# Sum of reciprocals: 127 rows a partition, and the last 128 rows loaded early onto chosen partitions

## The chip, the core and the metric

The kernel runs on one core of a Trainium2 chip. The metric is the device time of one execution in microseconds (us): the median of several runs. Lower is better.

## The reference

```python
batch, seq, dim = 32, 512, 1024
x = np.abs(np.random.randn(batch, seq, dim)).astype(np.float32) + 1e-6

def reference(x):
    return np.sum(1.0 / x, axis=-1).astype(np.float32)
```

There are 32 x 512 = 16,384 rows of 1,024 numbers (4,096 bytes a row, 67.1 MB in all). Each row gives one sum of reciprocals.

## The kernel before

**Layout.** 128 partitions hold 128 rows each: partition p has rows 128 p to 128 p + 127 of x. "Row r" below is the r-th row of all partitions at once, a 128 x 1,024 tile of 512 KB. A load (line 187, issued by SyncE, SP) brings one or several rows into `ring`, which has space for R = 40 rows; row r sits in place r % 40. The last two rows are loaded as halves (256 KB each), numbered 126 to 129. The ring is all the buffering there is: a load into a place waits until the row there before has been used up.

**Arithmetic.** A row is cut into halves a and b of 512 columns. Since 1/a + 1/b = (a + b) / (a b), one reciprocal serves two numbers. The reciprocal is made on ScalarE as exp(-ln(S a b)) with S = 2^17, and the factor S is put back in the last step. For every row there are these steps, each a letter in the plan:

- P (line 199): the product a b on GpSimd (POOL), mostly of two rows in one instruction, into a slot of `prod`. Some rows have it on VectorE (DVE, line 220) instead: W reads both halves from the ring, V reads b from PSUM, where a TensorE matmul with the identity (C, line 209) has copied it.
- L (line 242): Ln on ScalarE (ACT), in place in `prod`.
- E (line 251): Exp on ScalarE, in place, or into a bank of PSUM.
- S (line 232): for a part of the rows, two matmuls with the identity add a + b in a PSUM bank.
- R (line 267): one DVE instruction multiplies and sums. With S it takes (a + b) from PSUM and the reciprocal from `prod` (512 columns); without S it takes a and b from the ring and the reciprocal from PSUM (1,024 columns). It writes the row's sum into a column of `sums`, and frees the ring.

**Order.** `PLAN` is a list of some 500 such steps, written out by hand or by a planner; D is a load of so many rows. Every engine does its own steps in the order of the list. Loads are large at first (2, 10, 14, 14, 11, 9 rows) and small at the end (single rows, then halves), so that compute, which begins late, can catch up. The helper `note` keeps the waits between engines few. SP's loads use eight semaphores in turn, so a load also waits for the landing of the load eight places before it.

**Output.** When the sums of the first DONE = 114 columns are there, six stores of 19 columns go out (line 289), and a last one of 14 columns at the end (line 291).

Of the kernel before, what the change touches and what calls it, by code (L numbers as in the profile page):

```python
# [11 lines left out]
def kernel(  # L12
# [7 lines left out]
    P = 128  # L20
    D = 1024
    H = D // 2
    F = 128
    R = 40
    NP = 22
    LAST = F - 2
    DONE = 114
    S = float(2**17)

    PLAN = """
        D2 D10 D14 D14 P0+2 C3@3 S2@0 V3 P2 L0+2@0 C11@3 S3@1 E0+2@6 P4+2 V11 L2+2@2 R0 S6@2
        E2+2 R1 P6+2 L4+2@4 R2 R3 E4+2@6 S7@0 P8+2 L6+2@8 R4 S10@1 E6+2 R5 P10 L8+2@10 R6 R7  # L40
        S11@2 E8+2@6 L10+2@6 R8 E10+2 R9 D11 R10 R11 P12+2 C19@3 S14@0 V19 P14+2 L12+2@12
        S15@1 E12+2@6 S18@2 R12 P16+2 L14+2@16 R13 E14+2 R14 P18 L16+2@18 R15 S19@0 E16+2@6
        P20+2 L18+2@14 R16 S22@1 E18+2 R17 D9 P22+2 L20+2@20 R18 R19 E20+2@6 S23@2 P24+2
        L22+2@0 R20 E22+2 R21 L24+2@2 R22 R23 E24+2@6 P26 C27@3 R24 S26@0 P28+2 V27 R25 D7
        L26+2@4 C35@3 E26+2 S27@1 P30+2 V35 L28+2@8 R26 S30@2 R27 E28+2@6 P32+2 L30+2@10 R28
        S31@0 E30+2 R29 P34 L32+2@12 S34@1 R30 R31 E32+2@6 P36+2 S35@0 L34+2@6 R32 E34+2 R33
        D7 P38+2 S38@2 L36+2@16 R34 R35 E36+2@6 S39@1 P40+2 L38+2@18 R36 C43@3 E38+2 R37 D6
        S42@0 P42 L40+2@14 V43 R38 E40+2@6 P44+2 R39 S43@2 L42+2@20 R40 E42+2 S46@1 R41 D3
        P46+2 L44+2@0 R42 R43 E44+2@6 S47@0 P48+2 L46+2@2 R44 S50@2 E46+2 R45 P50 L48+2@4
        R46 C51@3 R47 E48+2@6 S51@1 P52+2 V51 R48 D6 L50+2@8 C59@3 E50+2 R49 P54+2 S54@0  # L50
        L52+2@10 V59 R50 E52+2@6 R51 S55@2 P56+2 L54+2@12 R52 E54+2 S58@1 R53 D5 P58
        L56+2@16 R54 R55 E56+2@6 S59@0 P60+2 L58+2@6 R56 S62@2 E58+2 R57 D4 P62+2 L60+2@14
        R58 R59 E60+2@6 S63@1 P64+2 L62+2@18 R60 S66@0 E62+2 R61 D4 P66 L64+2@20 R62 C67@3
        R63 E64+2@6 P68+2 S67@2 V67 R64 L66+2@0 S70@1 R65 D4 E66+2 P70+2 L68+2@2 R66 R67
        S71@0 E68+2@6 P72+2 L70+2@4 R68 D3 E70+2 R69 D2 C75@3 P74 L72+2@10 S74@2 R70 V75
        P76+2 E72+2@6 R71 S75@1 L74+2@8 R72 D2 E74+2 R73 D2 P80 S78@0 L76+2@12 R74 P81
        L80@16 R75 S79@2 E76+2@6 P78+2 L81@17 R76 D2 S81@1 E80@5 E81 R80 L78+2@6 W82 E78+2
        R81 R77 D1 D1 D1 D1 D1 P88 C85@6 S85@1 R78 P83 L88@18 V85 E88@7 R79 P84 S84@0
        L82+2@14 R88 E82+2@5 P86+2 L84+2@19 R82 D1 E84+2 R83 D1 D1 D1 C90@7 P91 L86+2@0
        S91@2 R85 P93 V90 E86+2@5 R84 P92 S90@1 L90+2@2 R87 L93@21 W89 L92@10 R86 D1 D1 D1  # L60
        D1 E93@7 P94 S97@0 E92@6 R93 E90+2 P97 S94@3 L89@11 R92 E89@7 P95 L97@8 R91 S95@4
        E97 R90 L94+2@4 W96 R97 P101 C99@6 L96@9 R89 E94+2 S100@0 P98 V99 E96@5 L101@12 R95
        P100 S99@1 L98@13 R96 E101@7 L99+2@16 R101 E98@6 P104 C103@5 R94 E99+2 S105@2 R98
        P102 L104@18 V103 E104@7 W105 L102+2@6 R100 P107+2 C106@6 L105@14 R104 E102+2@4
        S108@0 V106 E105 R102 L106+3@19 P109 S107@3 R103 P110 E106+3 R105 S106@4 R99 P111+2
        L109+2@0 R107 S112@1 R108 E109+2@6 R106 L111+2@10 P114 R109 S111@0 E111+2 R110 P113
        L114@15 R111 C115@7 P116 L113@2 R112 E114@6 V115 E113@5 S117@0 P117 R114 L116@3
        L115@8 P118 E116@7 R113 S118@1 E115@6 P119 L117+2@12 R116 E117+2 R115 P120 S120@2
        L119@9 R117 P121 L120@4 S121@3 R118 E119@7 E120 R119 P122 L121@5 S122@0 E121 R120
        P123 L122@18 R121 E122 W124 L123@6 R122 L124@7 W125 S125@1 E123@7 E124@6 R123 P126  # L70
        L125@14 P127 L126@16 S127@0 R124 E125 P128 L127@17 S128@2 E126@7 P129 R125 E127
        S129@3 L128@19 R126 L129@20 E128 R127 E129 R128 R129
    """.split()

    Ln = mybir.ActivationFunctionType.Ln
    Exp = mybir.ActivationFunctionType.Exp
    mult = mybir.AluOpType.mult
    add = mybir.AluOpType.add

    x_v = x.flatten_outer_dims().rearrange("(p f) d -> p f d", p=P)  # L80
    out_v = out.flatten().rearrange("(p f) -> p f", p=P)

    act_sets = list(get_activation_tables(nc.m.arch).keys())
    nc.scalar.add_instruction(  # L84
# [13 lines left out]
    prod = pool.tile([P, NP, H], f32)  # L98
    sums = pool.tile([P, F], f32)
    ident = pool.tile([P, P], f32)  # L100
    ps = pspool.tile([P, 8, H], f32)
    make_identity(nc, ident)

# [28 lines left out]
    begun = {}  # L132
    count = {}

    def note(engine, inst, reads=(), writes=()):
        inst = inst.ins
        known = dict(begun.get(engine, {}))
        before = {}
        for spaces, writing in ((reads, False), (writes, True)):
            for space in spaces:  # L140
                for other in history.get(space, ()):
                    if writing or other[3]:
                        before[other[0].name] = other
        needed = sorted(before.values(), key=lambda o: -o[4])
        for other in needed:
            o_inst, o_engine, o_tick, _, _, o_known = other
            if o_engine == engine:
                continue
            if o_tick <= known.get(o_engine, 0):
                tc.declare_no_dep(inst, o_inst, reason="implied by other waits")  # L150
                continue
            for e, t in o_known.items():
                known[e] = max(known.get(e, 0), t)
            known[o_engine] = max(known.get(o_engine, 0), o_tick)
        count[engine] = count.get(engine, 0) + 1
        begun[engine] = known
        entry = (engine, count[engine])
        if engine == "SP":
            entry = (f"load {count[engine]}", 1)
        for spaces, writing in ((reads, False), (writes, True)):  # L160
            for space in spaces:
                history.setdefault(space, []).append(
                    (inst, *entry, writing, sum(count.values()), known)
                )
# [10 lines left out]
    def slots(r, n):  # L175
        return [("slot", pslot[q]) for q in range(r, r + n)]

    with tc.manual_schedule():
        for op, r, n, b in ops:
            p = pslot.get(r)  # L180
            if op == "D":
                n, r = r, loaded
                while n:
                    q, at, w = place(r)
# [59 lines left out]
            elif op == "E":  # L244
                pg = prod[:, p : p + n, : place(r)[2]]
                rc = pg
                if b is not None:
                    rc = ps[:, b : b + n, : place(r)[2]]
                    for j in range(n):
                        bank[r + j] = b + j  # L250
                inst = nc.scalar.activation(out=rc, in_=pg, func=Exp, scale=-1.0)  # L251
                if b is None:
                    note("ACT", inst, writes=slots(r, n))
                else:
                    banks = [("bank", b + j) for j in range(n)]
                    note("ACT", inst, slots(r, n), banks)
            elif op == "R":
                q, at, w = place(r)
                other = ps[:, bank[r], :w]
                if r in halves:  # L260
                    row = prod[:, p, :w]
                else:
                    row = ring[:, q % R, at : at + 2 * w]
                    row = row.rearrange("p (h e) -> p h e", h=2)
                    other = other.unsqueeze(1).to_broadcast([P, 2, w])
                total = sums[:, q : q + 1]
                inst = nc.vector.tensor_tensor_reduce(  # L267
                    out=row,
                    in0=row,
                    in1=other,  # L270
                    scale=S,
                    scalar=total if q in summed else 0.0,
                    op0=mult,
                    op1=add,
                    accum_out=total,
                )
                summed.add(q)
                note(
                    "DVE",
                    inst,  # L280
                    [("bank", bank[r])],
                    slots(r, 1) if r in halves else rows(r, 1),
                )

                left.discard(r)
                if not left:
                    for c in range(0, DONE, DONE // 6):
                        part = slice(c, min(c + DONE // 6, DONE))
                        nc.sync.dma_start(out=out_v[:, part], in_=sums[:, part])
                    left.add(-1)  # L290
        nc.sync.dma_start(out=out_v[:, DONE:], in_=sums[:, DONE:])
# [30 lines left out]
```

## Time and profile before

| | us |
|---|---|
| median of 3 runs | 168.01 (167.95 to 168.02) |
| span of the profiled execution, first to last instruction | 166.3 |
| busy time, PE / DVE / ACT / POOL | 132.5 / 128.3 / 132.3 / 128.2 |
| DMA packets, per DMA engine | 95.6% of the span |
| POOL product, two rows (2 x 512 columns) | 2.34 |
| DVE product, 512 columns | 0.69 |
| DVE R, 512 / 1,024 columns | 0.68 / 1.21 |
| ACT pass, 512 / 1,024 columns | 0.61 / 1.06 |
| PE matmul 128 x 512 at full clock | 0.43 |

The profiled execution has no time of its own beside its span; the median of the runs is 1.7 us above the span, which is what lies around the first and the last instruction. The profile's rows name an engine, a line and the tiles (out<-in); "idle before" is an engine's idle time ahead of an instruction with what ended it. A DMA's issue is on SP, its data move on 16 DMA engines, and a load has landed when all sixteen have reported.

### The profile page before, as it was taken

To read this page: it belongs to the slowest core of one execution; us is meant where nothing else is said; L and a number is where in the kernel's file an instruction comes from. 1 tells how busy PE (TensorE), PEld (TensorE's weight loads), DVE (VectorE), ACT (ScalarE), POOL (GpSimd) and SP (SyncE) were. 2 spreads that over 40 slices of the span, in tenths; PEclk is the share of its full clock that TensorE was granted. 3 is DMA by queue.
4 is the path that set the end of the run, shared out by engine and by line. 5 is a ranking of instruction groups with operands and counts; after the bars stand their busy time and mean duration, and the time that the engine had idled before them with its cause. 6 is when DMAs were issued, how large, how long until landed. Compare 5 with 4: busy or idle time off the path is not lost.

```text
span 166.3 us, 1348 instructions
## 1 busy us (share of the span) xinstructions
PE 132.5 (80%) x292; PEld 55.2 (33%) x292; DVE 128.3 (77%) x282; ACT 132.3 (80%) x157; POOL 128.2 (77%) x81
## 2 busy tenths in 40 slices
PE   0000799978855999999999999988699979989982
PEld 0000333333312444444343433324234424433351
DVE  0000119885787699898998898989899999999994
ACT  3040073949995899999799999996999999999992
POOL 1500795069995999999999999948977869999860
PEclk9999999999996999999999999999999999999999
DMA  5999999999998989999999999999999999999940
GB/s 189 536 394 394 441 441 441 441 441 441 441 441 349 509 368 446 430 417 438 441 434 434 406 426 446 429 424 424 414 437 437 414 410 428 410 409 410 400 139 4
DMA packets 5768, 67.26 MB, mean 404 GB/s; under 512 B 1536, under 2 KB 1536, under 8 KB 3200
## 3 DMA queue, kind: packets, MB, share of 16 engines
q1 hardware_dynamic: 5760, 67.18, 95.6%
q8 instruction: 2, 0.03, 0.1%
q14 instruction: 6, 0.05, 0.1%
HBM read 67.11 MB, written 0.07 MB: 404 GB/s over the span
## 4 chain that ended last, share of the span: by engine, by line
DMA 57%; PE 18%; ACT 8%; DVE 6%; POOL 6%; issue 3%; SPq 1%; ACTq 0%; POOLq 0%; DVEq 0%
DMA ring<-in_x_dram 57%; PE ps L232 15%; POOL prod L199 6%; ACT prod L242 4%; PE ps L209 3%; ACT ps L251 2%; DVE ring L267 2%; DVE prod L267 2%; ACT prod L251 2%; DVE prod L220 1%; SPq L187 1%; DVE sums L267 0%; ACTq L242 0%; POOLq L199 0%; DVEq L317 0%
## 5 line engine op out<-in xcount | busy, mean ns | idle before, releaser
L199 POOL TENSOR_TENSOR prod<-ring 128x1024 f32<-128x1024 f32 (+2 forms) x75 | 127.5, 1727 | 33.5 <-DMA ring<-in_x_dram 27.1
L232 PE MATMUL ps<-ring,ident 128*128 128x512 f32 (+1 forms) x260 | 116.9, 596 | 5.2 <-DVE sums L267 4.5
L242 ACT ACTIVATE prod<-prod 128x1024 f32<-128x1024 f32 (+2 forms) x78 | 68.5, 892 | 24.9 <-DVE prod L220 14.3
L267 DVE CUSTOM_DVE_ANT_1 ring<-ring,ps 128x1024 f32<-128x1024 f32 (+1 forms) x65 | 76.4, 1208 | 8.9 <-ACT ps L251 8.7
L232 PEld LDWEIGHTS ps<-ring,ident 128*128 128x128 f32 x260 | 49.2, 193 | 71.7 <-issue 51.6
L267 DVE CUSTOM_DVE_ANT_0 prod<-prod,ps 128x512 f32<-128x512 f32 (+1 forms) x63 | 40.9, 677 | 0.4 <-PE ps L232 0.4
L209 PE MATMUL ps<-ring,ident 128*128 128x512 f32 x32 | 19.3, 689 | 25.7 <-DMA ring<-in_x_dram 24.0
L251 ACT ACTIVATE ps<-prod 128x1024 f32<-128x1024 f32 (+2 forms) x41 | 34.1, 838 | 4.5 <-DVE sums L267 3.7
L251 ACT ACTIVATE prod<-prod 128x1024 f32<-128x1024 f32 (+3 forms) x37 | 34.4, 931 | 0.9
L220 DVE TENSOR_TENSOR prod<-ring,ps 128x512 f32<-128x512 f32 x16 | 10.9, 684 | 26.3 <-PE ps L209 26.3
L209 PEld LDWEIGHTS ps<-ring,ident 128*128 128x128 f32 x32 | 6.0, 213 | 36.0 <-issue 21.4
L267 DVE DVE_READ_ACCUMULATOR2_ANT sums<- 128x1 f32 x130 | 10.7, 82 | 0.0
L220 DVE TENSOR_TENSOR prod<-ring 128x512 f32<-128x512 f32 x6 | 4.1, 688 | 0.1
L84 ACT ACT_TABLE_LOAD x1 | 1.3, 1283 | 0.7 <-PEq L306 0.7
L267 DVE CUSTOM_DVE_ANT_0 prod<-prod,ps,sums 128x256 f32<-128x256 f32 x2 | 0.9, 475 | 0.0
masks.py:197 POOL MEMSET ident<- 128x128 f32 x1 | 0.2, 204 | 0.3 <-POOLq L306 0.3
masks.py:199 POOL TENSOR_SCALAR_AFFINE_SELECT ident<-ident 128x128 f32<-128x128 f32 x1 | 0.3, 292 | 0.1
L306 POOL MEMSET const-float32-0.0<- 128x1 f32 x1 | 0.1, 98 | 0.2 <-issue 0.2
L306 POOL MEMSET const-bfloat16-1.0<- 128x1 bf16 x1 | 0.1, 101 | 0.0
L306 POOL MEMSET const-uint8-127<- 128x1 uint8 x1 | 0.1, 101 | 0.0
L306 POOL MEMSET const-float32-1.0<- 128x1 f32 x1 | 0.1, 98 | 0.0
## 6 DMA issues: line engine op xcount, KB each, us to landing
ring<-in_x_dram SPq DMA_DIRECT2D x2, 7168.0 KB, 41.2
ring<-in_x_dram SPq DMA_DIRECT2D x2, 3584.0 KB, 29.3
ring<-in_x_dram SPq DMA_DIRECT2D x2, 3072.0 KB, 31.9
ring<-in_x_dram SPq DMA_DIRECT2D x3, 2048.0 KB, 34.0
ring<-in_x_dram SPq DMA_DIRECT2D x1, 5632.0 KB, 30.3
ring<-in_x_dram SPq DMA_DIRECT2D x5, 1024.0 KB, 31.8
ring<-in_x_dram SPq DMA_DIRECT2D x1, 5120.0 KB, 16.5
ring<-in_x_dram SPq DMA_DIRECT2D x1, 4608.0 KB, 30.7
```

The lines of the kernel that those rows point to most:

```text
L84: nc.scalar.add_instruction(mybir.InstLoadActFuncSet(name=nc.get_next_instruction_name(), act_func_set_id=act_sets.index("natural_log_exp_ ...
L187: inst = nc.sync.dma_start(out=ring[:, a : a + m, at : at + 2 * w], in_=x_v[:, q : q + m, at : at + 2 * w],)
L199: inst = nc.gpsimd.tensor_tensor(out=prod[:, p : p + m, :w], in0=ring[:, a : a + m, at : at + w], in1=ring[:, a : a + m, at + w : at + 2 * w],
L209: inst = nc.tensor.matmul(ps[:, b, : place(r)[2]], lhsT=ident, rhs=xs(r, 1), start=True, stop=True,)
L220: inst = nc.vector.tensor_tensor(out=prod[:, p, :w], in0=xs(r, 0), in1=in1, op=mult)
L232: inst = nc.tensor.matmul(ps[:, b, : place(r)[2]], lhsT=ident, rhs=xs(r, h), start=h == 0, stop=h == 1,)
L242: inst = nc.scalar.activation(out=pg, in_=pg, func=Ln, scale=S)
L251: inst = nc.scalar.activation(out=rc, in_=pg, func=Exp, scale=-1.0)
L267: inst = nc.vector.tensor_tensor_reduce(out=row, in0=row, in1=other, scale=S, scalar=total if q in summed else 0.0, op0=mult, op1=add, acc ...
L306: nc = _bacc.Bacc("TRN2", target_bir_lowering=False, num_devices=1)
```

## The change

The partitions now hold F = 127 rows each (rows 0 to 16,255 of x), and the ring R = 39. The other 128 rows of x are "extra" rows, treated apart and early.

- 104 of them go as whole rows, one to a partition, into a new tile `extra`, in runs of partitions listed in `RUNS`. Two runs (partitions 0-7 and 32-39) are issued by SP between the first two loads, five (44-75, 84-95, 12-31, 96-107, 116-127) by GpSimd. Four very small GpSimd loads between them (`None` in the list, 2 or 3 numbers of 4 bytes) go to a tile that nothing reads. Partitions 8-11, 40-43, 76-83 and 108-115 get no whole extra row; they keep the value 1.0 that a DVE memset puts into `extra` before all these loads.
- The last 24 rows are cut in quarters: 96 partitions get 256 columns each, in one load from SP.
- The sums of the extra rows are made like the others (steps K4 to K9, after row 7): two products on DVE, Ln and Exp on ACT over 640 columns, two R instructions into `esums`. A 0/1 matrix `pick`, made on GpSimd (K3: two memsets and nine selects), brings the partitions' sums in the rows' order and adds the quarters, by two small matmuls (K10). DVE copies the 128 numbers out of PSUM (K11), and one store writes them (K12, on SP between two loads).
- The first two rows' products move from GpSimd (`P0+2`) to DVE (`W0 W1`).
- The fourth load has 13 rows instead of 14. From row 11 on, the plan is the one before with every row number one lower, apart from PSUM banks and slots and from loads that stand a place or two elsewhere in the list, some of them a row larger or smaller.

```diff
-    F = 128
-    R = 40
+    F = 127
+    R = 39
     NP = 22
-    LAST = F - 2
-    DONE = 114
+    LAST = 125
+    DONE = 113
+    EXTRA = P * F
+    Q = D // 4
+    RUNS = [
+        (0, 2, 0, "hw"),
+        (32, 2, 8, "hw"),
+        (None, 3, None, "sw"),
+        (44, 8, 16, "sw"),
+        (None, 2, None, "sw"),
+        (84, 3, 48, "sw"),
+        (None, 3, None, "sw"),
+        (12, 5, 60, "sw"),
+        (96, 3, 80, "sw"),
+        (None, 2, None, "sw"),
+        (116, 3, 92, "sw"),
+    ]
+    QUARTERS = 104
+    NQ = (P - QUARTERS) * 4
     PLAN = """
-        D2 D10 D14 D14 P0+2 C3@3 S2@0 V3 P2 L0+2@0 C11@3 S3@1 E0+2@6 P4+2 V11 L2+2@2 R0 S6@2
-        E2+2 R1 P6+2 L4+2@4 R2 R3 E4+2@6 S7@0 P8+2 L6+2@8 R4 S10@1 E6+2 R5 P10 L8+2@10 R6 R7
-        S11@2 E8+2@6 L10+2@6 R8 E10+2 R9 D11 R10 R11 P12+2 C19@3 S14@0 V19 P14+2 L12+2@12
+        K0 K1 D2 K2 D10 D14 D13 W0 W1 K3 C3@0 S2@1 V3 P2 L0+2@0 C10@2 S3@3
+        E0+2@4 P4+2 V10 L2+2@2 R0 S6@6 E2+2 R1 P6+2 L4+2@4 R2 R3 E4+2@4 S7@7
+        P8+2 L6+2@7 R4 E6+2 R5 L8+2@9 R6 R7 K4 K5 K6 K7 K8 K9 K10@0 K11 S10@2
+        E8+2@3 L10@6 R8 E10 R9 D11 R10 P11+2 C18@1 S13@5 V18 P13+2 L11+2@11
...
+    extra = pool.tile([P, D + Q], f32)
+    esums = pool.tile([P, 2], f32)
+    eout = pool.tile([1, P], f32)
+    skip = pool.tile([4, 4], f32)
+    pick = pool.tile([P, 2, P], f32)
...
+        if r == 0:
+            inst = nc.vector.memset(extra, 1.0)
...
+        elif r == 1:
+            for p0, n, row, by in RUNS:
...
+                if p0 is None:
+                    inst = nc.gpsimd.dma_start(
+                        out=skip[:n, j : j + 1], in_=x_e[:n, j : j + 1]
+                    )
+                else:
+                    inst = nc.gpsimd.dma_start(
+                        out=extra[p0 : p0 + 4 * n, :D],
+                        in_=x_e[row : row + 4 * n, :].rearrange("(j g) d -> g j d", g=n),
+                    )
...
+        elif r == 2:
+            for p0, n, row, by in RUNS:
+                if by == "hw":
+                    inst = nc.sync.dma_start(
+                        out=extra[p0 : p0 + 4 * n, :D],
+                        in_=x_e[row : row + 4 * n, :].rearrange("(j g) d -> g j d", g=n),
+                    )
...
+            inst = nc.sync.dma_start(
+                out=extra[:NQ, D:],
+                in_=x_e[QUARTERS:, :].rearrange("r (q e) -> (r q) e", q=4),
+            )
...
+        elif r in (6, 7):
+            pg = ep[:, : at[1][1]]
+            func, scale = ((Ln, S), (Exp, -1.0))[r - 6]
+            inst = nc.scalar.activation(out=pg, in_=pg, func=func, scale=scale)
...
+        elif r == 10:
+            for i in range(2):
+                inst = nc.tensor.matmul(
+                    ps[:1, b, :P],
+                    lhsT=esums[:, i : i + 1],
+                    rhs=pick[:, i, :],
+                    start=i == 0,
+                    stop=i == 1,
+                )
...
+        elif r == 12:
+            inst = nc.sync.dma_start(out=out_e, in_=eout)
```

## The prediction

> **What bounds the kernel now.** The page comes first: its shares, the DMA slices, the queues and the chain.
>
> ```profile
> PE 132.5 (80%) x292; PEld 55.2 (33%) x292; DVE 128.3 (77%) x282; ACT 132.3 (80%) x157; POOL 128.2 (77%) x81
> ...
> PEclk9999999999996999999999999999999999999999
> DMA  5999999999998989999999999999999999999940
> ...
> q1 hardware_dynamic: 5760, 67.18, 95.6%
> q8 instruction: 2, 0.03, 0.1%
> q14 instruction: 6, 0.05, 0.1%
> ...
> DMA 57%; PE 18%; ACT 8%; DVE 6%; POOL 6%; issue 3%; SPq 1%; ACTq 0%; POOLq 0%; DVEq 0%
> ```
>
> The DMA engines are full from the second slice to the last but two: 95.6% of the span of 166.3 is 159.0 us of packets an engine. Four compute engines are near 80%. So I look at the chain in order of time for who holds the end.
>
> ```profile
> 101.96 35.20 DMA ring<-in_x_dram
> ...
> 147.18 10.17 DMA ring<-in_x_dram
> 157.34 0.02 issue
> 157.37 0.38 DVE prod L220
> ...
> 163.63 0.39 DVE prod L267
> ```
>
> Loads hold it up to 157.34; then 6.65 us of DVE work end at 164.02, and the last output and exit make 166.3. A load issued at 101.96 lands 35 us later because the queue is full, not because it was issued late. Next, how compute stands to that, by windows.
>
> ```profile
> 35.00:40.00 5.00, 5.00 (x13) 2.17 (x12) 2.61 (x8) 2.69 (x3) 5.00 (x3) 1.00 0.85 367
> 40.00:45.00 5.00, 3.61 (x9) 1.35 (x8) 4.00 (x9) 4.72 (x6) 5.00 (x3) 1.00 1.27 551
> 45.00:50.00 5.00, 3.01 (x7) 0.87 (x5) 4.51 (x11) 4.94 (x6) 4.91 (x3) 1.00 0.85 367
> 50.00:55.00 5.00, 3.40 (x5) 1.61 (x6) 4.05 (x10) 2.53 (x3) 3.31 (x2) 0.66 0.99 425
> 55.00:60.00 5.00, 5.00 (x13) 2.13 (x13) 3.38 (x8) 4.91 (x6) 5.00 (x4) 1.00 1.00 433
> ...
> 120.00:125.00 5.00, 4.64 (x12) 1.87 (x11) 5.00 (x11) 4.97 (x8) 3.86 (x4) 1.00 1.02 436
> ```
>
> The third to seventh figures are length, PE, PEld, DVE, ACT, POOL. DVE idles 6.45 us from 35 to 60 (25 less 18.55), and later hardly: its records show no gap over 0.15 us from 117.55 to the end. POOL, in contrast, starts at 112.85, 123.81, 128.71, 133.61 and 137.29, each time 0.13 us after a load's last landing, having idled 1.1 us or more. So late in the kernel two limits lie side by side: the landings, and DVE's unbroken work.
>
> **What lands late.** The trace has sixteen landings a load, one a DMA engine. The load of 51.56 has them within 0.38 us. Then the instruction packets of q14 and q8 come (52.42, 69.64, 78.18, 109.44, 111.23, 140.84, 157.74), and engines fall behind one at a time: the load that ends at 77.06 has one landing 0.67 us behind the next. At 157.34 eleven stand at 155.36 to 155.75, two at 156.12 and 156.14, three at 157.04, 157.15 and 157.34. A load counts when its last landing is in, so three engines set the time and eleven are 1.6 us early.
>
> **The change, part by part.** *Bytes of each engine.* A 14-row packet of 57,344 B took 2,116 ns, 151 ns a row; a single 4,096 B row 162; half a row 84, so a quarter is between 38 (151/4) and 84, and I take 46, the row's rate plus the 8 ns that the half shows above its own share. Load 4 loses a row: 8 x 151 = 1.21 us less on every engine. Thirteen gain 8 single rows (1.30) and 6 quarters (0.28): net +0.37. The runs leave out partitions 8-11, 40-43, 76-83 and 108-115, 24 of them, three engines' share: these gain quarters alone, net -0.93.
>
> *Landings, if the three are the late ones.* At 51.56 nothing is late: 51.93, a loss of 0.37. At 112.72 the two late ones go from 112.72 to 111.79 and the next from 111.47 to 111.84: gain 0.88. At 157.34: 156.41 against 156.14 + 0.37 = 156.51, gain 0.83. The last load (160.54) has a fourth engine at 160.05 after the packet of 157.74: 160.42, gain 0.12.
>
> [...]
>
> *SP's queue.* Behind the 2-row load stand now two 8-partition runs and the quarters; the first waits for a DVE memset of 1,280 columns. No row shows one: POOL's memset of 128 columns took 0.20, a 512-column DVE product 0.69, so between 0.2 and 1.72 us, and I take 1.3, nearer the DVE row. From 0.75 it ends at 2.05 (worst 2.5). Three issues of 0.42 put the fifth DMA, the 10-row load, at 3.3 (worst 3.8); the first issue took 1.0 us to its first packet, so 4.3 to 4.8, and the 2-row load runs until 4.82. Cost 0; without that cover (issues of 0.8, the longest in the trace) 1.1 us of starved engines, which the early runs fill on thirteen. The small output put between two loads at 50 us is one issue of 0.33 under 30 us of queue: 0.
>
> *POOL's queue.* Nine DMAs of its own (those into the extra tile wait for the same memset), then 11 small instructions (3 us at the 0.29 of its select), stand ahead of its first product, which was at 5.66 and is now the one of row 2. The trace has no POOL-issued DMA: at least 0.33 (SP's issue), and 2.34 (POOL's longest usual instruction) as the other end; I take 1.0, toward SP's row. POOL is free from 1.3 until the 10-row load lands, at 17.7 plus about 1.3 for the early runs ahead of it: 17.7 us against 12. At 2.34 it would be 6.4 us late, and its idle 7.50 us from 27.18 would take that.
>
> *Compute of the extra rows.* On DVE: two products for POOL's first (1.37, in idle time), then after row 7 products of 512 and 128 columns (0.69 + 0.3), reduces of 1,024 and 256 (1.21 + 0.5, and 0.16 for accumulators), a 128-column copy (0.3): 3.2 us. Between them it waits for two 640-column ACT passes (0.72 each, between the 0.61 of 512 and the 1.06 of 1,024) and for two matmuls with loads (0.8): 5.4 us altogether; a gain is excluded, as work is only added, and with the copy and the short product at 0.69 it is 6.2. One row's reduce leaves (1.14). With landings 1.3 later that is about 5.6 of the 6.45 us idle. ACT has 5.12 idle from 35 to 55, against 1.44 plus its waits. The cover nearly suffices; I let 0.2 us through. Queued behind this chain on DVE are the reduces of rows 8 to 10, which free the ring for the 11-row load; it was issued at 35.13 and the queue was full until 51.56, so 5 us later starves nothing. From row 11 on the order is the old one with row numbers one lower, loads moved by a place or two, so nothing after it has less to do.
>
> *Sum.* ACT starts its unbroken stretch (54.50 to 112.82) 0.37 + 0.2 later, ends at 113.4, and takes up the load of 111.84 after POOL at 113.28 instead of 114.16: gain 0.76 there. DVE was free at 116.89 and waited until 117.55; free at 117.46 it gains 0.1, or the full 0.65 if the early delays vanish. A reason that they do: PE's clock in the windows above is 0.66 of full at 50:55 after PE's idle 2.70 us, and 128x512 matmuls took 1.04 instead of 0.43; that puts 1.4 us on the PE chain and makes ACT wait 0.83 at 79.0. With early rows about 3 us later PE no longer idles so long. [...] I take most of it: 0.57 late less 0.6, DVE 0.6 earlier at 117.55, inside the 0.83 of 157.34. The last landing came 1.0 us before POOL took it up (its four half-row products run from 159.43 to 162.23 in one piece, the last from 161.5), so its small gain of 0.12 holds nothing back. Gain 0.6: span 165.7. The median 168.01 lies 1.7 above this span; left as it is, 167.4.
>
> **Rivals.** *A, the gain does not get through* (DVE keeps its 117.55, or early lateness eats it): 0.1 to 0.3, 167.7 to 168.2. For it: DVE's unbroken stretch; against: POOL's and ACT's waits for landings. *B, slower:* the three left out are not the late ones. Then the landings of 112.72 and 157.34 move by +0.37; from any mapping in which one late engine carries extra rows this decides: 168.4, and with 0.57 of early lateness 168.6. For it: the trace names no engine; against: three are late by 1.6 us and three get 1.30 less. *C, slower:* the extra rows' chain on DVE outgrows its cover: past the 6.45 us of idle every us goes to ACT's stretch and on to DVE; at 8 us DVE is free at 116.89 + 0.37 + 1.55 = 118.81 instead of 117.55: 169.3, and 168.7 with the clock's 0.6. *D, more:* ACT and DVE both free and the fourth engine not late: 0.9 to 1.2, 166.8 to 167.1.
>
> **Chances.** Forecast 0.45 (167.1 to 167.65), D 0.13, A 0.17, B 0.14, C 0.11. This kernel's runs can tell 0.2% (0.34 us) from no change: faster 0.58, the same 0.17, slower 0.25. Leaving out the far end of D and C beyond one us, the range is 166.7 to 168.8.
>
> **What would show it.** Right: landings of a load within 1.1 us late in the trace, POOL's starts at about 111.9 and 136.4, first landing of load 4 near 51.9, the fifth SP DMA without a DMA gap at 4.8, PE's clock at full at 50:55. Wrong: three landings 2 us behind (B); DVE or ACT idle gone and PE waiting for DVE at 52 to 60 (C); DVE still at 117.5 (A).

## The result and the profile after

The changed kernel takes 183.13 us (median of 4 runs, 181.86 to 186.35); the kernel before takes 168.01. The ratio is 1.087 (interval 1.083 to 1.091): 15 us slower, where 0.6 us faster was predicted. The profiled execution took 183.2 with a span of 181.5. (Runs more than 1.5% above the fastest of the same kernel are left out of the ratios; where a kernel's runs fell into two groups, both are given.)

The page of the kernel after, its rows for busy time, clock, DMA, queues and chain:

```profile
PE 129.6 (71%) x292; PEld 55.7 (31%) x292; DVE 136.4 (75%) x290; ACT 132.1 (73%) x159; POOL 133.5 (74%) x100
...
PEclk9999999975558999999999999999999999999996
DMA  6999999998985999999999999999999999997000
...
q1 hardware_dynamic: 5894, 66.82, 89.3%
q0 software_dynamic: 528, 0.36, 0.6%
...
DVE 29%; DMA 21%; ACT 19%; POOL 18%; issue 9%; PE 2%; DVEq 0%; POOLq 0%; ACTq 0%
```

DMA held 57% of the chain before; now DVE, ACT and POOL hold most of it, and loads are done three slices before the end instead of one. There is a hole in the DMA row at the thirteenth slice, and PE's clock is at half from 38.4 to 55.5 us. Busy time has grown on DVE by 8.1 us. A new queue, q0, carries the loads that POOL issues: 0.6% of the engines' time. The chain in order of time says what that small queue does:

```profile
6.23 0.15 issue
6.38 37.65 DMA extra<-in_x_dram
44.03 0.02 issue
44.06 4.43 DVE prod L285 x2
...
50.05 1.23 DVE extra L301
```

The last run of extra rows (partitions 116 to 127, 48 KB) is on its way from 6.38 to 44.03. DVE's first product of the extra rows (K4) stands in DVE's order behind row 7 and waits for it. Windows of the same stretch as before (length, PE, PEld, DVE, ACT, POOL, clock, DMA share, GB/s):

```profile
35.00:40.00 5.00, 0.00 (x0) 0.00 (x0) 1.78 (x6) 1.17 (x2) 0.00 (x0) 0.84 0.98 384
40.00:45.00 5.00, 0.00 (x0) 0.00 (x0) 0.94 (x1) 0.00 (x0) 4.05 (x2) 0.50 1.00 427
45.00:50.00 5.00, 0.00 (x0) 0.00 (x0) 3.48 (x2) 1.46 (x3) 4.61 (x3) 0.50 0.99 426
50.00:55.00 5.00, 3.67 (x7) 1.42 (x8) 4.13 (x9) 3.06 (x5) 3.64 (x2) 0.50 0.79 341
55.00:60.00 5.00, 5.00 (x13) 2.28 (x12) 3.97 (x8) 4.90 (x5) 5.00 (x4) 0.95 0.80 288
```

PE has no work for 15 us, ACT almost none, while everything waits for DVE. The row-8 reduce (R8) starts at 52.59; before, it started at 32.65. The 19.9 us between them add up from the trace: row 7 was done at 36.77, 4.1 after the time at which R8 began before (the 10-row load landed at 22.45 instead of 17.68); DVE waited 7.3 for the run; the two products took 2.08 + 2.42 = 4.4; DVE waited 1.57 for ACT's two passes; the two reduces took 1.57; PE's matmuls and the copy 0.97. Of these 19.9 us, 4.5 were made good by the rows that DVE has at 60 us in the kernel before and at 76 in the kernel after, and then hardly anything: rows of DVE run 14.8 to 15.8 later than before from there to the end. In the stretch from 60 to 110 DVE has the same work in the same time, first after, then before:

```profile
60.00:110.00 50.00, 50.00 (x118) 22.23 (x117) 45.77 (x102) 47.08 (x48) 49.84 (x25) 1.00 0.99 427
```

```profile
60.00:110.00 50.00, 49.10 (x112) 20.46 (x111) 45.79 (x102) 48.18 (x50) 49.53 (x25) 1.00 1.00 427
```

So the loss is made before 60 us, and less than a quarter of it is won back. Two things about it were open: why the run lands so late, and how much of the 15 us hangs on it.

### The profile page after: what moved, and what is told of

It reads as the page before. It is cut to its first block, busy times and chain, and to the rows that moved or that the text cites. A ratio compares the mean times of both kernels' runs of the same rounds, so it can differ in the third digit from the quotient of the medians.

```text
span 181.5 us, 1411 instructions
## 1 busy us (share of the span) xinstructions
PE 129.6 (71%) x292; PEld 55.7 (31%) x292; DVE 136.4 (75%) x290; ACT 132.1 (73%) x159; POOL 133.5 (74%) x100
## 4 chain that ended last, share of the span: by engine, by line
DVE 29%; DMA 21%; ACT 19%; POOL 18%; issue 9%; PE 2%; DVEq 0%; POOLq 0%; ACTq 0%
DMA extra<-in_x_dram 21%; POOL prod L354 15%; DVE ring L422 14%; ACT prod L397 10%; DVE prod L422 7%; ACT ps L406 5%; DVE prod L375 4%; ACT prod L406 3%; DVE prod L285 2%; PE ps L387 2%; POOL extra L231 1%; POOL skip L227 1%; DVE sums L422 1%; ACT prod L295 1%; DVE extra L301 1%
## 5 line engine op out<-in xcount | busy, mean ns | idle before, releaser
L354 POOL TENSOR_TENSOR prod<-ring 128x1024 f32<-128x1024 f32 (+2 forms) x74 | 125.6, 1729 | 34.5 <-DMA ring<-in_x_dram 30.0
L387 PE MATMUL ps<-ring,ident 128*128 128x512 f32 (+1 forms) x256 | 115.0, 599 | 3.2 <-DVE sums L422 3.1
L364 PE MATMUL ps<-ring,ident 128*128 128x512 f32 x32 | 18.0, 644 | 23.9 <-DMA ring<-in_x_dram 22.6
L295 ACT ACTIVATE prod<-prod 128x640 f32<-128x640 f32 x2 | 1.5, 737 | 12.4 <-DVE prod L285 12.3
L285 DVE TENSOR_TENSOR prod<-extra 128x512 f32<-128x512 f32 (+1 forms) x2 | 4.4, 2248 | 7.3 <-DMA extra<-in_x_dram 7.3
L375 DVE TENSOR_TENSOR prod<-ring 128x512 f32<-128x512 f32 x8 | 6.5, 821 | 3.4 <-DMA ring<-in_x_dram 3.4
L231 POOL DMA_DIRECT2D extra<-in_x_dram x5 | 2.8, 568 | 0.1
L301 DVE CUSTOM_DVE_ANT_1 extra<-extra,prod 128x1024 f32<-128x1024 f32 (+1 forms) x2 | 1.6, 824 | 1.6 <-ACT prod L295 1.6
L227 POOL DMA_DIRECT2D skip<-in_x_dram x4 | 2.3, 574 | 0.4 <-issue 0.4
L219 DVE MEMSET extra<- 128x1280 f32 x1 | 1.1, 1125 | 1.2 <-PEq L462 1.2
```

What stands on the lines that cost most here:

```text
L227: inst = nc.gpsimd.dma_start(out=skip[:n, j : j + 1], in_=x_e[:n, j : j + 1])
L231: inst = nc.gpsimd.dma_start(out=extra[p0 : p0 + 4 * n, :D], in_=x_e[row : row + 4 * n, :].rearrange("(j g) d -> g j d", g=n),)
L285: inst = nc.vector.tensor_tensor(out=ep[:, at[i][0] : at[i][1]], in0=eh[i][:, 0, :], in1=eh[i][:, 1, :], op=mult,)
L295: inst = nc.scalar.activation(out=pg, in_=pg, func=func, scale=scale)
L301: inst = nc.vector.tensor_tensor_reduce(out=eh[i], in0=eh[i], in1=rc, scale=S, scalar=0.0, op0=mult, op1=add, accum_out=esums[:, i : i + 1],)
L354: inst = nc.gpsimd.tensor_tensor(out=prod[:, p : p + m, :w], in0=ring[:, a : a + m, at : at + w], in1=ring[:, a : a + m, at + w : at + 2 * w],
```

## Experiments

In every edit only the changed lines of the kernel after are shown. "Even" is short for the extra rows as one load of all 128 partitions.

### The wait for the last run: e1_late and e3_half

e1_late moves the chain behind row 22, where the run has long landed:

```diff
-... R6 R7 K4 K5 K6 K7 K8 K9 K10@0 K11 S10@2
+... R6 R7 S10@2
-... R21 R22 E23+2@1 P25 C26@7 R23 S25@0 P27+2 V26 R24 L25+2@2 C34@4
+... R21 R22 K4 K5 E23+2@1 K6 K7 P25 C26@7 R23 S25@0 P27+2 K8 K9 V26 R24 L25+2@2 K10@3 K11 C34@4
```

> The changed kernel with the extra rows' compute (K4 to K11) taken out from behind row 7 and put behind row 22, where DVE and ACT waited for the fourth load before. Loads and GpSimd-issued runs as in the changed kernel. Theory 1, the loss is DVE's wait for the last GpSimd-issued run (until 44.06 us), with all that stands behind it: that wait is gone, the 11-row load is issued near 41 us as the queue still has work, and the time is 167.4 to 168. Theory 2, the GpSimd-issued packets also make the large packets beside them slower (40,960 B took 1.70 us instead of 1.51, 57,344 B 2.24 instead of 2.12) and so delay the whole load stream: the fourth load lands near 56 us as in the changed kernel instead of 51.6, the queue never runs dry after that, and the time is 171 to 173, of which nothing can be won back, since the DMA engines are full to the end.

Measured: 183.99 (ratio 1.093, 1.090 to 1.097). Both theories miss. DVE did not wait for the run, the 11-row load went out at 38.67 and the DMA queue did not run dry; but rows came 6.2 us late on DVE before the chain (45 to 57 us), and 13.4 after it (from 68 us on). The products took 2.55 + 2.42 us there and the reduces 1.73 + 1.47. So the wait is not the only way to lose: loads were about 5 us late anyway (the fourth load's last landing 56.6, before 51.56), and a chain of 7 us among full DVE work costs its whole length.

e3_half keeps the chain where it is and cuts the large loads beside which the runs travel:

```diff
-        K0 K1 D2 K2 D10 D14 D13 W0 W1
+        K0 K1 D2 K2 D5 D5 D7 D7 D7 D6 W0 W1
```

> The changed kernel with the loads of 10, 14 and 13 rows issued as 5+5, 7+7 and 7+6 (packets half as long, the same bytes), nothing else changed. Theory of one packet in turn (a small packet of the GpSimd queue goes after each large packet of the SP queue on the same engine, some 20 packets in all): the last GpSimd-issued run lands near 25 to 29 us instead of 44, before DVE comes to K4 at about 37, DVE's wait is gone and the time is 170 to 173. Rival, the runs are late for another reason (GpSimd's own issue, the order of its semaphores): they still land near 44 and the time stays near 183.

Measured: 173.77 (1.033, 1.031 to 1.035). The last run landed at 25.8, K4 waited for nothing, and 9.4 of the 15 us are back. R8 starts 10.0 earlier than in the kernel after: the 7.3 of waiting are gone, row 7 is done 3.6 earlier (33.14), as the first rows landed earlier too, the products took 0.6 less and the reduces 1.5 more. So e3_half shows what late landings cost together, and not the wait for the last run alone. The rows of DMA issues of the kernel after, of e3_half and of e9 (below; 2-row loads), with the median time from issue to landing of the three 48 KB runs:

```profile
extra<-in_x_dram POOLq DMA_DIRECT2D x3, 48.0 KB, 25.7
```

```profile
extra<-in_x_dram POOLq DMA_DIRECT2D x3, 48.0 KB, 13.9
```

```profile
extra<-in_x_dram POOLq DMA_DIRECT2D x3, 48.0 KB, 9.5
```

The same loads, 26, 14 or 9.5 us, by what lies beside them. In the trace of after, rows of the last run start at 34.37, 36.75 and 39.15, spaced as on one engine: one small packet, then one packet of a large load (about 2.2 us), then the next small one. A packet of SP's large loads is 40 to 57 KB here and took, in the median, 1.70 us at 40,960 B and 2.24 at 57,344 B. Between 6.4 and 44 us the 16 engines start 296 packets of the large loads, 18 to 19 each (37.0 us of packets an engine), and 317 packets of POOL's queue, 20 each; at one small packet between two large ones, that is the 38 us.

### An even load: e2_even and e4_even_tiny

e2_even takes the runs and the nine POOL DMAs away, nothing else:

```diff
-    RUNS = [ (0, 2, 0, "hw"), ... (116, 3, 92, "sw") ]
+    RUNS = [(0, 32, 0, "even")]
...
+            inst = nc.sync.dma_start(out=extra[:, :D], in_=x_e)
```

> The changed kernel with its 128 extra rows in one ordinary load from SP, one row on each of the 128 partitions (so the same bytes for every DMA engine), no GpSimd-issued loads, no quarters; K4 to K11 stay behind row 7. Both theories of the GpSimd-issued runs: K4 starts when DVE gets there (33 to 35 us) without a wait for loads, the fourth load lands near 51.7 us, the time is 168.0 to 168.6 (nothing won on late engines). Rival C of the prediction, the chain of extra compute is too long for DVE's idle time: 169 or more, with ACT or PE waiting for DVE between 50 and 60 us. Two-input products on DVE (K4, K5), which took 2.08 and 2.42 us while GpSimd was in products: 0.69 and about 0.2 here if GpSimd is idle then.

Measured: one run of 169.83, five of 173.3 to 174.0 (the profile is of the second group). K4 started without a wait (34.11), but the chain took 7.1 us, because one short reduce stalled: see below. The fourth load landed at 52.80. e4_even_tiny adds nine 4-byte DMAs from POOL to it:

> As the even load (128 extra rows in one SP load), with nine GpSimd-issued loads added that move 4 bytes to each of 2 to 8 partitions into a tile that nothing reads. If packets of a second queue cost by their number and not their bytes: 40,960 B and 57,344 B packets take 0.1 to 0.2 us longer while they last, the fourth load lands 2 to 3 us later than with the even load alone, and the time is 170 to 171. If it is the 4 KB rows that cost: as the even load, within 0.3 us.

Measured: two runs of 169.9 (ratio 1.010), two of 173 and 174. The 4-byte DMAs landed one after the other until 32.5 us, but large packets kept their 1.514 and 2.116 us and the fourth load landed at 52.81. Small packets as such took nothing from the others here. In the kernel after, however, the same large packets took 1.70 and 2.24 us while runs were in flight; that comes up again with e9.

### Where the chain stands, and SP's wait: e5_early_even and e17_early_even_nowait

e5 puts the chain into the idle time of the first load:

```diff
-... W0 W1 K3 C3@0 S2@1 V3 P2 L0+2@0 C10@2 S3@3
+... W0 W1 K3 L0+2@0 K4 K5 K6 K7 K8 K9 K10@7 K11 C3@0 S2@1 V3 P2 C10@2 S3@3
```

> Like e2_even (extra rows as one even 128-partition load, nothing issued from POOL), but the whole chain of the extra rows stands behind the first two DVE products, ahead of the product of row 3, that is in the 12 us in which DVE, ACT and POOL wait for the 10-row load. Theory 1, the place of the chain is what cost the 4 to 5 us there: DVE, ACT and POOL are idle, so its 6 to 7 us end by about 14, before the load lands at about 20; DVE at row 60 is late by no more than the loads are (1.2), PE's clock has its half-speed stretch at 51 to 54 as before, and the time is 168.4 to 169.6 (before, plus the 1.24 us by which the fourth load was late in e2_even, less what is hidden). Rival, the extra rows' DVE work must be paid wherever it stands because DVE, ACT and PSUM are one loop to the end: 172 to 174 as in e2_even.

Measured: 169.63 (1.009, 1.0075 to 1.011): theory 1, at its upper end. The chain ran from 7.56 to 12.73, 5.2 us. The same DVE instructions in three kernels: products (L285) in after and e5, reduces (L301) in e2 and e5; count, busy and mean ns, idle before:

```profile
L285 DVE TENSOR_TENSOR prod<-extra 128x512 f32<-128x512 f32 (+1 forms) x2 | 4.4, 2248 | 7.3 <-DMA extra<-in_x_dram 7.3
```

```profile
L301 DVE CUSTOM_DVE_ANT_1 extra<-extra,prod 128x1024 f32<-128x1024 f32 (+1 forms) x2 | 3.7, 1895 | 1.6 <-ACT prod L295 1.6
```

```profile
L301 DVE CUSTOM_DVE_ANT_1 extra<-extra,prod 128x1024 f32<-128x1024 f32 (+1 forms) x2 | 1.6, 823 | 1.6 <-ACT prod L295 1.6
...
L285 DVE TENSOR_TENSOR prod<-extra 128x512 f32<-128x512 f32 (+1 forms) x2 | 0.9, 486 | 0.7 <-DMA extra<-in_x_dram 0.7
```

In e5 POOL does nothing at that time, and the two products take 0.69 and 0.28. In after POOL is inside its two-row products (43.25 to 45.59 and 45.54 to 48.32), and they take 2.08 and 2.42. The 256-column reduce takes 0.42 in e5 and 2.56 in e2. All four read both inputs from SBUF. Most of the kernel's other DVE work takes one input from PSUM; the sixteen products of that kind take 0.68 to 0.69 in after, thirteen of them wholly beside products of POOL. The exception is six products of ring rows (step W) late in the kernel. POOL is idle beside them in before but for 0.13 us of one, and all six take 0.68 to 0.69; in after two begin in the middle of a product of POOL and take 1.29 and 1.16, and one begins 0.15 us before the end of one and takes 0.70. The ends go together in the trace of after: these three products end at 127.90, 138.92 and 152.38, each 0.55 us behind a product of POOL (127.35, 138.37, 151.83); K4 ends at 46.13, 0.54 behind 45.59, and K5, of 128 columns, at 48.48, 0.16 behind 48.32. So these products of DVE waited here for the end of POOL's; what makes them wait is not shown. The rows of before and of after (there with W0 and W1, which make eight):

```profile
L220 DVE TENSOR_TENSOR prod<-ring 128x512 f32<-128x512 f32 x6 | 4.1, 688 | 0.1
```

```profile
L375 DVE TENSOR_TENSOR prod<-ring 128x512 f32<-128x512 f32 x8 | 6.5, 821 | 3.4 <-DMA ring<-in_x_dram 3.4
```

e17 shortens the memset that SP's second DMA waited for:

```diff
-            inst = nc.vector.memset(extra, 1.0)
+            inst = nc.vector.memset(extra[:, D:], 1.0)
```

> e5_early_even (169.63) with the DVE memset cut to the columns that no load fills (1,024 to 1,279), so that SP's load of the extra rows, which fills all 128 partitions, no longer waits for it. Theory: SP's wait of 1.1 us goes, the fourth load lands at 51.4 instead of 52.27, and the time falls by 0.8 to 1.1 to 168.5 to 168.8: the best form of the extra rows found here, and still not below before, since the bytes are the same on every engine. Rival: the DMA engines had enough to do and nothing changes.

Measured: 168.93 (1.0044, 1.0030 to 1.0058), 0.1 above the forecast, fourth load 51.73 instead of 52.27. SP's wait costs 0.5 us of landings and 0.7 of time. DVE is only 0.2 late at the end; the rest is an end of the program that is 0.65 us longer (last section).

### What the runs themselves cost: e6 to e10

e6 and e9 are a pair in one order, with the first twelve rows as 2-row loads, so that runs land early; e6 has the even load, e9 the change's runs (the e7 that the expectations name gave no time; e9 stands in its place). e8 is the kernel before with the same loads.

```diff
-        K0 K1 D2 K2 D10 D14 D13 W0 W1 ...
+        K0 K1 D2 D2 K2 D2 D2 D2 D2 D14 D13 W0 W1 K3 L0+2@0 K4 K5 K6 K7 K8 K9 K10@7 K11 ...
```

> e5_early_even with the first 12 rows loaded as six 2-row loads, the extra rows' load behind the second of them, so that SP has something to issue while it waits for the memset. It is the even half of a pair with e7_early_runs_d2, which has the same order and differs only in where the extra rows' bytes go. Theory: DMA engines do not run dry at 4 us any more, the fourth load lands 1.0 to 1.2 us earlier than in e5 (51.6 to 51.9), rows 2 to 11 come in turn from 6 us on, and the time is 167.4 to 168.4. Rival: the chain now meets POOL's products of the early rows, its two-input DVE instructions take 2.0 to 2.6 us each, and rows that came early wait behind it: 169 to 171.

> The kernel before, with its 2-row and 10-row load as six 2-row loads and nothing else changed: the control for e6 and e7. Theory: the end is set by the landings of the last loads, which a finer split of the first 12 rows does not move; 167.6 to 168.2, the same. Rival: earlier rows shift the whole DVE, ACT and POOL loop forward and the time falls by 0.5 or more.

> The change's own runs (two from SP, nine DMAs from POOL, quarters) in the order of e6_early_even_d2 (168.70, span 166.8): the first twelve rows in six 2-row loads, the chain of the extra rows behind the first two DVE products. Behind 2-row packets the small ones of the POOL queue wait 0.35 us each instead of 1.5, so the last run lands by 10 to 14 us. Theory 1 (the prediction's byte balance works once nothing of the chain is late): against e6 the spread of a load's landings after 110 us is 0.6 to 1.3 smaller, the late landings are 0.5 to 0.9 earlier, and the time is 167.8 to 168.3. Rival 1: what makes engines late has nothing to do with the engines that were spared, and landings and time are those of e6 within 0.3. Rival 2 (rival B of the prediction): the late engines carry extra rows; 169.0 to 169.6.

Measured: e6 168.70 (1.0034, 1.0022 to 1.0045), between the two values; e8 169.40 (1.0073, 1.0061 to 1.0085), neither "the same" nor a gain; e9 171.92 (1.027, 1.022 to 1.032; four runs near 171.9, two at 174.0), above all three values. With the same order of work, the runs still cost 3.2 us against the even load (171.92 - 168.70). This is the price of the whole bundle: in e9 the last run lands at 17.43, and DVE's chain begins at 17.51 instead of 9.54. That late chain is not what costs, since in e19 (below) the last run lands at 16.89 and the time is 169.18, 2.7 less than e9. In e9 the fourth load's landings are at 53.55 to 55.60, in e6 at 51.58 to 52.05: even the first engine is 2 us late, although by the prediction's sum three engines had 0.93 us less. And the sixteen landings are not thirteen and three: fourteen lie within 0.95 us, two stand at 1.83 and 2.05. e10 makes the first 4-byte DMA one element longer, which by the list's own reckoning moves all later POOL runs on by one engine:

```diff
-        (None, 3, None, "sw"),
+        (None, 4, None, "sw"),
```

> e9_early_runs_d2 with one more 4-byte element in the first of the small POOL DMAs (4 instead of 3), which by the kernel's own reckoning moves all POOL-issued rows on by one DMA engine: one engine that carries a run from SP now gets 16 extra rows, and of the three that were to be spared two get 8. If the spared engines are the late ones (theory 1 of e9), the late landings are 1.3 later than in e9 or more and the time 0.9 to 1.4 longer. If the late engines are others or change, or if the rows do not go one group to an engine, the time is e9's within 0.3.

Measured: 172.05, the same time and the same picture (fourteen within 0.91, two at 1.77 and 2.08).

### Why packets grow: e13 to e16, e18, e19

e13 issues e6's even load from POOL; e14 issues e9's runs from SP and drops the 4-byte DMAs; e15 is e6 with the rows in the runs' strided order; e16 is e6 with the extra rows in two loads of 64 partitions; e18 has four POOL loads of 32 partitions, e19 six of 32, 32, 20, 12, 12 and 20.

```diff
e13 -            inst = nc.sync.dma_start(out=extra[:, :D], in_=x_e)
e13 +            inst = nc.gpsimd.dma_start(out=extra[:, :D], in_=x_e)
e15 +            ... in_=x_e.rearrange("(j g) d -> g j d", g=32)
e16 +            for p0 in (64, 0):
e16 +                inst = nc.sync.dma_start(out=extra[p0 : p0 + 64, :D], in_=x_e[p0 : p0 + 64])
e18 +    RUNS = [(p, 8, r, "sw") for p, r in ((0, 0), (64, 32), (32, 64), (96, 96))]
e19 +    RUNS = [(0, 8, 0, "sw"), (64, 8, 32, "sw"), (32, 5, 64, "sw"), (52, 3, 84, "sw"), (96, 3, 96, "sw"), (108, 5, 108, "sw")]
```

> e6_early_even_d2 (168.70) with the one even load of the extra rows issued from POOL instead of SP; nothing else differs. It tells apart why every packet grew while the change's runs were in flight (8,192 B: 0.309 us in e6, up to 0.45 in e9). If rows issued from POOL do it, the packets grow here too, the 2-row loads of 8 to 16 us come about 2 us later, the fourth load lands at 53.5 to 55.5 and the time is 170 to 172. If it is the placement of the rows (four partitions a group, out of order), packets stay at 0.309, the fourth load lands near 52, and the time is 168.5 to 169.3.

> e9_early_runs_d2 (171.92) with all seven runs issued from SP in one queue with the loads and the 4-byte DMAs left out; same partitions, same order inside a run. The other half of the pair with e13. If the placement or the shape of the runs lengthens packets, 8,192 B packets grow to 0.4 while the runs are in flight and the fourth load lands 54 to 56, time 171 to 172.5. [...]

> e6_early_even_d2 (168.70) with the even load's rows in the order of the change's runs (four neighbouring partitions take rows 32 apart), still one DMA of 128 partitions. If the order of the rows lengthens packets, 8,192 B packets of 8 to 12 us grow from 0.309 to 0.4 and the fourth load's last landing moves from 52.05 to 53 or later; if not, both stay within 0.2 and the time is 168.5 to 169.0.

> [...] If writing to another engine's partitions is what lengthens packets in the change's runs, 8,192 B packets grow to 0.35 to 0.45 while they are in flight and the fourth load lands 0.5 to 2 us later than in e6 (52.05); if it is the uneven number of rows an engine, packets and landings stay, and the time is 168.5 to 169.2.

> e13_early_even_pool (168.89) with the extra rows in four DMAs of 32 partitions from POOL, each in the form of the change's largest run (eight groups of four partitions), in the order 0-31, 64-95, 32-63, 96-127. If POOL's queue goes on from one DMA engine to the next across its DMAs, as the change's list of runs and 4-byte DMAs reckons, every engine then writes the partitions that it writes for the ring's loads: 8,192 B packets stay at 0.309, the fourth load lands near 52.1, time 168.7 to 169.2. If each such DMA begins at the same engine, eight engines get 16 rows each and write half of them to partitions of the other eight: packets grow to 0.4 and more, the fourth load's last landing comes 1.2 us later or more, time 170 to 172.

> e18_even_four (168.97) with its two later DMAs cut in two each, in the sizes of the change's smaller runs: 20, 12, 12 and 20 partitions (five, three, three, five groups of four), in the order of the engines. By the change's reckoning (one group to an engine, going on from the last) every engine still writes its own partitions: packets of 8,192 B stay at 0.309 and the time is 168.8 to 169.3. If POOL's DMAs of 12 and 20 partitions are not dealt out by groups of four, rows go to engines that do not own their partitions: packets grow to 0.35 to 0.45 while they are in flight (10 to 16 us), the fourth load's last landing comes 1 us later or more, and the time is 170 to 172, as in the change's runs (e9, 171.92).

Measured: e13 168.89, e15 168.75, e18 168.97, e19 169.18 (most of its runs 168.8 to 169.3): all like e6, 8,192 B packets at 0.309 us. e14 173.02 and e16 170.07 (1.011, 1.009 to 1.013) are not. Windows from 8 to 10 us, last two figures DMA share and GB/s, of e6, e9, e16 and e18 in turn:

```profile
8.00:10.00 2.00, 0.00 (x0) 0.00 (x0) 0.46 (x1) 0.08 (x1) 1.26 (x1) 1.00 1.06 444
```

```profile
8.00:10.00 2.00, 0.00 (x0) 0.00 (x0) 0.00 (x0) 0.09 (x1) 1.86 (x11) 1.00 1.07 309
```

```profile
8.00:10.00 2.00, 0.00 (x0) 0.00 (x0) 0.00 (x0) 0.00 (x0) 1.26 (x1) 1.00 1.10 250
```

```profile
8.00:10.00 2.00, 0.00 (x0) 0.00 (x0) 0.00 (x0) 0.05 (x1) 1.26 (x1) 1.00 1.04 432
```

The engines are fully busy in all four, but in e16 they move 250 GB/s instead of 444: its 8,192 B packets take 0.60 us, its 4,096 B rows 0.30 instead of 0.16. In e9 they take 0.43 and 0.22 in the median, up to 0.59 and 0.27. e16 differs from e6 in two ways: the load is cut in two, each into half of the partitions, and each half has 64 packets and sixteen landings, four rows an engine. That its engines write to partitions of another engine is what its expectation supposes; the trace names no engine, so no run shows it, and what two loads into half of the partitions do by themselves is not parted from it. Neither POOL's queue (e13), nor the order of rows (e15), nor small POOL loads as such (e18, e19) do it.

Whether the runs of the change reach the engines that its list reckons with is not shown either. By the list, thirteen engines get the same and three get less; in e9 fourteen landings lie together and two stand 0.9 us behind, and the longer 4-byte DMA of e10 left both the time (172.05 against 171.92) and this picture as they were. So the author's estimate is that the runs miss the engines of the list. In e18 and e19 there are no 4-byte DMAs between the loads, and packets stay at 0.309 us; what the 4-byte DMAs do to the place of the runs was not measured alone, and runs on thirteen engines without them were not tried.

e14's SP issues took 0.4 to 0.8 us each and the queue ran dry from 8 to 11 us, so only its longer packets (0.39 from 10 to 12 us) count here, not its time.

### PE's half clock: e11_after_warm and e12_even_warm

Both put matmuls that nothing reads into PE's idle time ahead of K10 (70 of them in after, 24 in e2):

```diff
-... K9 K10@0
+... K9 K13@0 K10@0
```

> The changed kernel with 70 more matmuls of 256 columns (identity by the selection matrix, into the PSUM bank that the extra rows' own matmuls overwrite next; about 0.22 us each, 15 us) on PE just ahead of the extra rows' matmuls, that is in the 17 us in which PE waits and after which its clock was at half for 17 us. Theory 1 (the half clock is a price of its own, about 4 us, as the two speeds of e2_even at clocks 0.977 and 0.96 suggest): no half-speed stretch after 50 us, time 178 to 180. Rival (the DVE chain's wait of 7.3 us and its slow products set all of the loss; PE has slack at half clock): 182 to 184, the same as the changed kernel.

> e2_even with 24 such matmuls (5.3 us) ahead of the extra rows' matmuls, in PE's idle time of 6.3 us. Theory 1: the clock of every run is that of the fastest run of e2_even (0.977) or above, and every run takes 169.5 to 170.3. Rival (the slower runs of e2_even come from elsewhere, DVE's products beside POOL's): most runs still at 173 to 174.

Measured: e11 197.92, e12 174.10. The filler took 0.43 us a piece (30.4 us for 70), not 0.22, so in e11 it outlasted the gap and DVE waited for it. The waits of e11 from 45 to 70 us (total, times, longest):

```profile
DVE eout L335 <- PE ps L315: 13.1, 1, 13.1
...
DVE prod L285 <- DMA extra<-in_x_dram: 7.4, 1, 7.4
```

As a test of the time the two failed. But PE's clock stayed full from 27.5 to 191 us in e11, and without the 13.1 us wait it would have taken 184.8, an estimate (197.92 less 13.1), no less than the changed kernel with 17 us at half clock. By this the half clock is not what costs, and runs of the kernel before say the same (below). Nor is it what parts e2's two groups: e12 had full clock and took 174.1, of which 1.5 is the longer wait for PE. What parts them stays open. In the profiled runs of e2 and e12, eight products with both inputs from the ring took 8.0 and 7.8 us, where those of e5, e6 and e17 took 5.4; that could be some 2.5 of the 4 us, but no run of e2's faster group has a trace.

## Why the prediction was wrong

**The step that failed.** In "POOL's queue" the nine DMAs were priced by their issue on POOL (1.0 us each; 0.52 to 0.71 measured) and by what they push back (1.3 us on the 10-row load, which landed 4.8 later instead). When they would land was never asked, though K4 waits for all of them. The answer, 44.03, is one large packet of waiting (1.70 to 2.24 us) for each small one. e3_half moves that by 18 us, and the first rows by 3.6, and gives 9.4 us back.

**The chain on DVE** was priced at 5.4 us; alone it takes 5.2 (e5). In its place it took 15.9: 7.3 of waiting, 3.5 more for products beside POOL, the rest as priced. The rows used for the price were of DVE products that read PSUM, or of times when POOL was idle. **The cover** of 6.45 us was partly real: 4.5 us of the 19.9 were made good there. Rival C had the right mechanism (past the cover every us goes through to the end), but at 8 us of chain, not 15.9: its price, 168.7 to 169.3, is 14 us from the change. That e5, e6 and e17 lie near it is a coincidence, since their chain stands elsewhere.

**The bytes.** Net +0.37 and -0.93 us an engine supposed that rows go where the list says, and that a row costs its own packet. The second failed: in e9 a row's packet takes up to 0.27 instead of 0.16. Landings of the fourth load are at 54.20 to 56.69 instead of 51.93, and in e9 no engine is early. Which engine writes which partitions, and so the -0.93 on three engines, no run shows; what e9 showed in its place is fourteen landings within 0.95 us and two at 1.83 and 2.05. The runs as a whole are worth 2.7 to 3.2 us (e9 less e19 or e6); e16's split alone costs 1.4. So rivals A and B, which engines are late at the end, were never put to the test. (The landing at 160.54 that the prediction calls the last load's is that of the third half-row load; the last one's is at 161.27. The sum does not rest on it.)

**SP's queue** was to cost 0 and costs 0.5 to 0.7 us (e17 against e5). The 11-row load "5 us later starves nothing": it went out 20.7 us later (55.86 instead of 35.13), and the engines lost 2.15 us each from 54 to 60. e1, without that hole, was no faster, so it does not set the time.

**PE's clock** was to give 0.6 us back. It has nothing to give: 18 runs of the kernel before with a mean clock of 1.000 take 167.98 to 168.49 (middle 168.20), 25 with 0.979 take 167.94 to 168.28 (middle 168.13). Matmuls in the slow stretch are longer (records of 1.06 us in after up to 55 us, 0.59 from 55.7 on), but no one at the end waits for it.

What is left of the plan: the extra rows as an even load with the chain in idle time and no wait on SP (e17, 168.93) are 0.4% slower than before, and with 2-row loads (e6, 168.70) 0.3%. No form tried here is faster.

## What to carry to other kernels

A load of small packets on another queue beside a queue of large ones landed here not after its bytes but after as many large packets as an engine has small ones (48 KB after 37.65 us): price its landing, then look who waits for it. A DVE product with two SBUF inputs took 2.08 us here beside POOL's products and 0.69 without them, so price it from a row in which POOL was working too. Extra rows in four or six POOL loads of 12 to 32 partitions left packets of 8,192 B at 0.309 us here (e18, e19), two loads of 64 partitions brought them to 0.60 (e16), so show in the trace, by packet durations, what a placement costs.

## What the runs showed of the hardware

- In after one packet of a POOL-issued load waited about one packet of SP's loads, 1.70 to 2.24 us at 40 to 57 KB: 38 us for 18 to 19 turns; 4-byte DMAs came one in 3 to 4 us (e4).
- Beside two 64-partition loads, packets of 8,192 B took 0.60 us instead of 0.309 beside one of 128 partitions, at a DMA share of 1.10 against 1.06 (8 to 10 us, e16 against e6). What in the two loads does it is not shown.
- DVE's 512- and 128-column products beside POOL's two-row products: 2.08 and 2.42 us instead of 0.69 and 0.28 (after against e5); its 256-column reduce 2.56 instead of 0.42 (e2 against e5). The sixteen products with one input from PSUM stay at 0.68 to 0.69 (after).
- The end of the program differs from kernel to kernel. From the last store's issue to the end of the span it is 2.25 us in before, 2.39 in e6, 2.35 in e9, and 2.90 in e8 and e17. It does not go by the number of DMAs (40 in before, 42 in e17, 44 in e8, but 46 in e6 and 57 in e9). In e8 SP waits for the last store's semaphore first and for four others behind it, 0.65 us in all, of which 0.43 is one wait. What sets it stays open; about half of e8's 1.2 us is this.
